# Second norm under the out projection, splits under the merge, solved rows copied by VectorE, inverses in runs of four, HGRN keys a step ahead

## The chip, the cores and the metric

The kernel runs on one core of a Trainium2 chip. The metric is the device time of one execution in microseconds (us): the median of three runs. One execution was also taken with the hardware profiler; the rows further down come from it. Engines: PE (TensorE, matrix products), DVE (VectorE), ACT (ScalarE), POOL (GpSimd), and SP, which here only issues DMAs from its queue.

## The reference, cut to what matters

One layer of a hybrid decoder for 1024 prompt tokens and 8 sample sequences of one token, model width 1024:

```python
h = _rms_norm(x, norm_mix_g)
p_rwkv, p_hgrn, p_gate = split(h @ w_in)          # 1792 | 2048 | 2048 columns
o_a = rwkv7_mixer(p_rwkv)       # 8 heads of 64, delta-rule matrix state, token by token
o_b = hgrn2_mixer(p_hgrn)       # 4 heads of 128, gated linear recurrence, chunks of 64
gate_a, gate_b = split(sigmoid(p_gate))
x = x + (gate_a * (o_a @ w_up_a) + gate_b * (o_b @ w_up_b)) @ w_out
h = _rms_norm(x, norm_ffn_g)
x = x + (silu(h @ w_ffn_gate) * (h @ w_ffn_up)) @ w_ffn_down
y = _rms_norm(x, norm_final_g)
```

The outputs are y for prompt and samples and the new states of both mixers.

## The kernel before, in words

**Data.** Activations stand transposed: 128 channels in the partitions, tokens along the free dimension. The tokens go through in two halves, half 0 with 512 tokens and half 1 with 512 and the 8 samples (520, in two pieces of 260). A tile of 128 channels by one half is the unit; eight of them are the model width (`KD` is 8).

**A dense product.** Precision comes from a split: a tile or a weight is written as high part plus low part (`split`: a copy by ACT rounds the high part, DVE or POOL subtracts for the low one), and `mm3` makes three products of each pair, high by high, low by high and high by low. A weight tile is loaded by `wload`: a DMA that SP issues, ACT's copy `wh`, POOL's subtraction `wl` in four pieces of 256 columns. A 128 x 260 product over eight tiles of the model width is thus 24 matmuls.

**Order of the work.** The program is written as generators. `push` puts a weight's products at the end of a stream of dense work; `start` adds a generator of other work (a chain of a mixer, a norm). `drive` takes the other work's step that is due first, and wherever that step is still waiting it runs one `dense_step` of the stream in the gap. `finish_stream` runs the rest of the stream without other work. Each `yield` is thus a place into which dense work may come. The framework's scheduler then sets each engine's instructions in one fixed order; an engine waits at the first instruction that is not ready.

**Mixers.** Each half has eight RWKV heads in pairs and four HGRN heads. For RWKV the token-by-token recurrence is solved in chunks: `rwkv_prep` inverts the small triangular matrices of all chunks (14 steps of substitution, two DVE operations each, on tiles with one matrix per partition; the data comes to that form and back by DMAs over DRAM, tiles `x`, `t`, `ubd`, `ebd`, `tbd`), and `rwkv_chain` goes through the chunks one after the other: products, the solved rows `z` of two heads copied from PSUM into one operand (`sz`, the trace's `vsz`), and from this operand the new state. `hgrn_chain` does the same over windows: `token_major` transposes a window's keys and values with two PE transposes and an ACT copy (`kv`), two products give the new state and the outputs.

**Tail of a half.** When the last chains are through, the merge of the half follows: `push_merge` pushes per output tile m the products with both `w_up` weights (four PSUM tiles per m in half 1), which DVE multiplies with the sigmoid gates (loaded by DMA) and adds into `merged[m]`. In half 1 the eight merged tiles are then split in `push_out`, which also pushes the out projection: eight weights `w_out`, per tile two PSUM tiles (`pd`) that DVE adds to x1. ACT squares that sum, and DVE adds the squares up for the norm. `second_norm` turns a half's x1 into the operands of the next stage, a Strassen-like form with sums and differences of quadrants: for each of four pairs of tiles four scalings (with PSUM operand), four sums or differences, and five splits of which POOL subtracts two. `second_norm(0)` runs as other work beside the merge of half 1. Then come the FFN (gate, up, by Strassen-like groups) and the down projection, whose operands and weights use slots of named pools (`gslots`).

## Time and profile before

| | us |
|---|---|
| median of three runs | 1928.99 |
| fastest of them | 1925.67 |
| profiled execution, its own time | 1921.57 |
| its span, first to last instruction | 1919.8 |

| engine | busy us | share |
|---|---|---|
| PE | 1772.6 | 92% |
| DVE | 1078.6 | 56% |
| POOL | 969.0 | 50% |
| ACT | 808.7 | 42% |

PE is the engine with the most work. Its idle time is read by stage: the mixers of half 0 and half 1 fill the first 1094 us of the span, the merge of half 1 runs from there to 1134 us, its out projection to 1198 us, and FFN and down projection to the end. In the rows further down, an entry such as `[13.03 <-ACT w__12090 L160]` says that the engine was idle for 13.03 us before this instruction and that ACT's write of `w__12090` ended that wait. Nearly all operations of DVE, ACT and POOL carry line 160, that of the wrapper that issues them, so they are told apart by the tiles' names. The granted clock is a share of TensorE's 2.4 GHz: 1.00 is that, 0.50 is 1.2 GHz.

### The profile page before, as it was taken

The numbers are of one execution on the slowest core, as the hardware profiler recorded it, in microseconds if no ns is written. First come the engines' busy times: TensorE is split into PE (matmuls) and PEld (weight loads), VectorE is DVE, ScalarE is ACT, GpSimd is POOL, SyncE is SP. The second block draws the span as 40 slices with busy tenths as digits, with TensorE's granted clock in tenths as the row PEclk, the third lists the DMA queues.
The fourth block names the chain that finished last, engine by engine and source line by source line (L and its number), as shares of the span: only waits on it lengthen the run. The fifth ranks groups of instructions, "written<-read, shape, count | busy, mean of one in ns | idle before, by whom it ended". The sixth has DMA issues, their size and how long they took to land. (4 is left out here: it accounts for less than half of the span.)

```text
span 1919.8 us, 32939 instructions
## 1 busy us (share of the span) xinstructions
PE 1772.6 (92%) x12376; PEld 1628.9 (85%) x12376; DVE 1078.6 (56%) x2315; ACT 808.7 (42%) x1601; POOL 969.0 (50%) x1131
## 2 busy tenths in 40 slices
PE   6998999988799799899889869999999999999997
PEld 5776778778678789788889769999999999889987
DVE  4476577657465366567554593856656665531214
ACT  4446556656342456354344453433333333421111
POOL 6545555645365456556364364654434343542342
PEclk9998999999899899889989889999999999999998
DMA  4233233343444225323434543123221322732212
GB/s 133 87 72 98 84 81 84 113 131 112 150 161 126 76 66 88 103 70 95 124 114 129 175 156 130 67 89 105 72 84 67 103 75 95 253 109 56 72 52 89
DMA packets 172304, 199.05 MB, mean 104 GB/s; under 512 B 99632, under 2 KB 108080, under 8 KB 172144
## 3 DMA queue, kind: packets, MB, share of 16 engines
q1 hardware_dynamic: 172144, 196.94, 34.3%
q8 instruction: 97, 1.59, 0.4%
q14 instruction: 63, 0.52, 0.1%
HBM read 156.30 MB, written 40.07 MB: 102 GB/s over the span
## 5 line engine op out<-in xcount | busy, mean ns | idle before, releaser
L160 ACT ACT_TABLE_LOAD x66 | 84.7, 1283 | 1.8 <-PEq L1825 0.7
L160 POOL TENSOR_TENSOR d__20102<-d__20102,d__20103 128x512 f32<-128x512 f32 (+1 forms) x14 | 14.2, 1016 | 21.3 <-ACT d__20103 L160 21.3
L160 DVE SCALAR_TENSOR_TENSOR w__6304<-p__6021,vec,pm__6305 128x512 f32<-128x512 f32 x1 | 0.7, 747 | 21.2 <-PE pm__6305 L238 21.2
L238 PE MATMUL pd__12144<-w__12090,wh__12128 128*128 128x260 f32 x1 | 0.6, 584 | 13.0 <-ACT w__12090 L160 13.0
L160 POOL TENSOR_TENSOR wl__1389<-w__1386,wh__1388 128x256 fp32r<-128x256 f32 x4 | 3.2, 841 | 17.0 <-ACT wh__1388 L160 17.0
L160 POOL COPY own<-wkv_st 64x64 f32<-64x64 f32 x16 | 6.2, 386 | 10.7 <-PE pm__4635 L238 3.3
L238 PEld LDWEIGHTS pd__12144<-w__12090,wh__12128 128*128 128x128 f32 x1 | 0.3, 288 | 13.2 <-ACT w__12090 L160 13.2
L160 POOL TENSOR_TENSOR wl__11476<-w__11473,wh__11475 128x256 fp32r<-128x256 f32 x4 | 3.7, 940 | 14.3 <-ACT wh__11475 L160 14.3
L238 PE MATMUL pm__219<-ones,t__196 128*128 128x1 f32 x4 | 1.0, 357 | 9.5 <-DVE t__196 L160 9.5
L160 POOL TENSOR_TENSOR wl__5125<-w__5122,wh__5124 128x256 fp32r<-128x256 f32 x4 | 3.6, 936 | 11.3 <-ACT wh__5124 L160 11.3
L160 POOL TENSOR_TENSOR wl__10054<-w__10051,wh__10053 128x256 fp32r<-128x256 f32 x4 | 2.8, 736 | 12.7 <-ACT wh__10053 L160 12.7
L160 POOL TENSOR_TENSOR wl__3944<-w__3941,wh__3943 128x256 fp32r<-128x256 f32 x4 | 3.3, 855 | 11.8 <-ACT wh__3943 L160 11.8
L238 PEld LDWEIGHTS pm__219<-ones,t__196 128*128 128x128 f32 x4 | 0.9, 322 | 9.5 <-DVE t__196 L160 9.5
L160 POOL TENSOR_TENSOR wl__12202<-w__12199,wh__12201 128x256 fp32r<-128x256 f32 x4 | 2.8, 734 | 11.2 <-ACT wh__12201 L160 11.2
L238 PE MATMUL pm__6333<-t__6313,ebd 128*128 128x128 f32 x8 | 2.1, 441 | 6.6 <-ACT t__6313 L160 6.6
L238 PEld LDWEIGHTS pm__6333<-t__6313,ebd 128*128 128x128 f32 x8 | 1.8, 328 | 6.8 <-ACT t__6313 L160 6.8
L238 PE MATMUL pm__5093<-w__4985,wh__5071 128*128 128x512 f32 x1 | 0.8, 792 | 7.3 <-ACT w__4985 L160 7.3
L160 POOL TENSOR_TENSOR wl__10209<-w__10206,wh__10208 128x256 fp32r<-128x256 f32 x4 | 2.8, 733 | 8.7 <-ACT wh__10208 L160 8.7
L160 POOL TENSOR_TENSOR wl__6274<-w__6271,wh__6273 128x256 fp32r<-128x256 f32 x4 | 2.8, 719 | 8.7 <-ACT wh__6273 L160 8.7
L160 POOL TENSOR_TENSOR wl__1106<-w__1103,wh__1105 128x256 fp32r<-128x256 f32 x4 | 5.1, 1291 | 4.0 <-ACT wh__1105 L160 4.0
L160 POOL TENSOR_TENSOR wl__11397<-w__11394,wh__11396 128x256 fp32r<-128x256 f32 x4 | 2.8, 732 | 7.9 <-ACT wh__11396 L160 7.9
L238 PE MATMUL pc__7693<-vsz__7629,kbt__7700 128*128 128x128 f32 x2 | 0.8, 500 | 6.4 <-ACT vsz__7629 L160 6.4
(23703 smaller groups left out, 8520.1 us busy)
## 6 DMA issues: line engine op xcount, KB each, us to landing
tbd<-t SPq DMA_DIRECT2D x32, 32.0 KB
w__166<-in_w_in SPq DMA_DIRECT2D x1, 512.0 KB
w__184<-in_w_in SPq DMA_DIRECT2D x1, 512.0 KB
w__452<-in_w_in SPq DMA_DIRECT2D x1, 512.0 KB
w__461<-in_w_in SPq DMA_DIRECT2D x1, 512.0 KB
w__501<-in_w_in SPq DMA_DIRECT2D x1, 512.0 KB
w__541<-in_w_in SPq DMA_DIRECT2D x1, 512.0 KB
w__581<-in_w_in SPq DMA_DIRECT2D x1, 512.0 KB
```

The costliest lines, as they stand in the source:

```text
L160: return f(*args, **kw)
L238: PE.matmul(out, lhsT, rhs, start=start, stop=stop)
```

## The change

Five things are moved; the counts of instructions stay, except that 64 copies 64 x 64 pass from ACT to DVE, and that ACT loads its function table 69 times where it was 66.

1. `rwkv_prep` yields after every second step of an inverse's substitution (runs of four DVE operations) in place of every fifth.
2. `rwkv_chain` has both copies of `z` done by DVE; one was ACT's.
3. `hgrn_chain` issues the transposes and the copy of the next window's keys and values right behind this window's products, without a step of its own.
4. In half 1 each merged tile is split as soon as its merge ends, into slots of pool `h` that are free by then, and the out projection follows at once. The sums of squares of half 0 stay beside the merge, while `second_norm(0)` runs beside the out projection of half 1.
5. The operands of the second norm and the down projection's tiles use other slots for that.

```diff
@@ -776,7 +776,7 @@
                 ALU.mult,
             )
             V.tensor_tensor(n3[:, 0:q, q + 1 : 16], n3[:, 0:q, q + 1 : 16], tv, ALU.add)
-            if q % 5 == 0:
+            if q % 2 == 0:
                 yield
         V.memset(nb[:, 0:256:17], 1.0)
         d2 = dp.tile([4 * nblk, 256], F32, tag="d2", name=nm("d2"))
@@ -924,8 +924,8 @@
                 kbt1 = token_major(c + 1)
             yield
             mm(z, tbd[:, c], d_)
-            V.tensor_copy(sz[HEADS[0], 1, 0], z[HEADS[0], 0])
-            A.activation(sz[HEADS[1], 1, 1], z[HEADS[1], 1], AF.Copy)
+            for h in range(2):
+                V.tensor_copy(sz[HEADS[h], 1, h], z[HEADS[h], h])
             yield
             mm(ds, kbt, sz[:, 1])
             for h in range(2):
@@ -1183,6 +1183,8 @@
             if s0 is not None:
                 mm(py, qe[:, wc], s0, True, False)
             mm(py, at[:, w], kv[:, 1], s0 is None, True)
+            if w + 1 < NWIN:
+                kv = token_major(w + 1)
             if s0 is None:
                 V.tensor_copy(sn, po[:, :P])
             else:
@@ -1192,9 +1194,6 @@
             V.scalar_tensor_tensor(at[:, w], yr[:, wc], 1.0, yr[:, wc], ALU.mult, ALU.mult, accum_out=ss[:, w : w + 1])
             s0 = sn
             yield
-            if w + 1 < NWIN:
-                kv = token_major(w + 1)
-                yield
         if half == 1:
             SP.dma_start(out=o["hgrn_p"][hd], in_=s0)
         u["y"] = yr, ss
@@ -1268,7 +1267,7 @@
             for b in range(2):
                 item(m, b)
 
-    def push_merge(m, half, src, gates, merged):
+    def push_merge(m, half, src, gates, merged, done=None):
         def body(w):
             y = merged[m]
             gs = [slot(HLEN[half], tag="t") for _ in range(2)]
@@ -1283,7 +1282,7 @@
                     V.tensor_tensor(g[:, sl], g[:, sl], ps, ALU.mult)
                 V.tensor_tensor(y[:, sl], gs[0][:, sl], gs[1][:, sl], ALU.add)
 
-        push(i["w_up"][m], body)
+        push(i["w_up"][m], body, done)
 
     def add_to(y):
         return lambda sl, ps: V.tensor_tensor(y[:, sl], y[:, sl], ps, ALU.add)
@@ -1361,7 +1360,9 @@
         mh, ml, rest = many(half, F32R)
         for m in range(KD):
             split(merged[m], mh[m], ml[m])
-
+        push_out_of(half, mh, ml, x1, done)
+
+    def push_out_of(half, mh, ml, x1, done=None):
         def item(m):
             push(
                 i["w_out"][m],
@@ -1371,7 +1372,6 @@
 
         for m in range(KD):
             item(m)
-        return mh + ml + rest
 
 
     xs = [slot(HP) for _ in range(KD)]
@@ -1444,8 +1444,9 @@
         pools[tag], bufs[tag], widths[tag] = fp, FSLOTS[tag], HP + NS
 
     merged = [slot(HLEN[1], tag="p") for _ in range(KD)]
+    mh, ml = h_slots(1)
     for m in range(KD):
-        push_merge(m, 1, src, s["gates"], merged)
+        push_merge(m, 1, src, s["gates"], merged, lambda m=m: split(merged[m], mh[m], ml[m]))
 
     x1 = [slot(HP, tag="p") for _ in range(3)]
     for _ in range(2):
@@ -1453,8 +1454,6 @@
     x1.append(slot(HP, tag="n"))
     for m in range(KD):
         SP.dma_start(out=x1[m], in_=x1d[m])
-    h2t = [[slot(HP, F32R, "h") for _ in range(16)] + [slot(HP, F32R, tag=y) for y in "w" * 11 + "n"], None]
-
     def operands(tiles, half):
 
         n = HLEN[half] // 2
@@ -1465,7 +1464,7 @@
         ops["B11"] = [[t[:, part * n : part * n + n] for t in tiles[6::7]] for part in range(2)]
         return ops
 
-    def second_norm(half, x1, acc, tiles):
+    def second_norm(half, x1, acc, tiles, b12=None):
         n = HLEN[half] // 2
         rs = rstd(acc, half)
         yield
@@ -1492,20 +1491,28 @@
             split(b1, h2, l2, G)
             yield
 
+    acc0 = slot(HP, tag="t")
+
+    def sums():
+        add = square_sum(acc0)
+        for k in range(KD):
+            add(x1[k])
+            yield
+
+    start("norm", sums())
+    drive()
+    finish_stream()
+
+    h2t = [[slot(HP, F32R) for _ in range(SLOTS["w"])], None]
+    for _ in range(2):
+        h2t[0] += parts_of(double(F32R), HP + NS)
+    for _ in range(2):
+        h2t[0] += parts_of(triple(F32R), HP + NS)
+    rest = h2t[0][7 * KD // 2 :]
+    h2t[0] = [y[:, :HP] for y in h2t[0][: 7 * KD // 2]]
     h2s = [operands(h2t[0], 0), None]
     b12 = [slot(HP, F32R, "s") for _ in range(KD // 2)]
-
-    def first_second_norm():
-        acc = slot(HP, tag="t")
-        add = square_sum(acc)
-        for k in range(KD):
-            add(x1[k])
-            yield
-        yield from second_norm(0, x1, acc, h2t[0])
-
-    start("norm", first_second_norm())
-    drive()
-    finish_stream()
+    x1_first = x1
     x1 = load_x(1, "pppppppp")
     x1e = dp.tile([KD, P, HLEN[1]], F32, tag="x1e", name="x1e", bufs=1)
     acc1 = slot(tag="n")
@@ -1516,10 +1523,13 @@
         for f, (a, b) in zip(add, CHUNKS[1]):
             f(x1[m][:, a:b])
 
-    h2t[1] = push_out(1, merged, x1, residual)
+    push_out_of(1, mh, ml, x1, residual)
+    start("norm", second_norm(0, x1_first, acc0, h2t[0], b12))
+    drive()
+    h2t[1] = mh + ml + rest
     for _ in range(2):
         h2t[1] += parts_of(double(F32R), HLEN[1])
-    h2t[1] += [slot(HLEN[1], F32R, "n") for _ in range(6)]
+    h2t[1] += [slot(HLEN[1], F32R, "n") for _ in range(7)]
 
 
 
@@ -1669,10 +1679,10 @@
                 yield from ts
 
     gslots = (
+        (("w", 16),),
+        (("h", 16), ("d", 8), ("n", 4)),
+        (("w", 19), ("a", 6), ("n", 3)),
         (("h", 16),),
-        (("n", 7), ("w", 13), ("d", 8)),
-        (("h", 16), ("w", 6), ("a", 6)),
-        (("w", 13), ("n", 3)),
     )
     x1s = [[slot(HP, tag="p") for _ in range(KD)], [slot(tag=y) for y in "pppttttt"]]
     f0s = [sum(FGROUPS[:g]) for g in range(len(FGROUPS))]
```

The order of the instructions on each engine shows what becomes of that at three places.

The first is the seam between the merge and the out projection of half 1. On PE before, `pd__12023` is the merge's last product, `pd__12144`, `pd__12170` and `pd__12208` are tiles of the out projection, and `w__12090` is the first merged tile's high part:

```order
L238 MATMUL pd__12023<-a__11298,wh__11886 128x260 x2
L238 MATMUL pd__12023<-a__11298,wl__11887 128x260
L238 MATMUL pd__12144<-w__12090,wh__12128 128x260
L238 MATMUL pd__12170<-w__12090,wh__12128 128x260
L238 MATMUL pd__12208<-w__12090,wh__12137 128x260
L238 MATMUL pd__12144<-w__12091,wh__12128 128x260
L238 MATMUL pd__12144<-w__12090,wl__12129 128x260
```

PE now; `pd__11973` is the merge's last product, `pm__12035` the sum of squares of half 0 and `pd__12062` the first out tile:

```order
L238 MATMUL pd__11973<-a__11298,wh__11851 128x260 x2
L238 MATMUL pd__11973<-a__11298,wl__11852 128x260
L238 MATMUL pm__12035<-ones,t__11367 128x1 x4
L238 MATMUL pd__12062<-h__11337,wh__12046 128x260
L238 MATMUL pd__12062<-h__11345,wh__12046 128x260
L238 MATMUL pd__12062<-h__11337,wl__12047 128x260
L238 MATMUL pd__12062<-h__11338,wh__12046 128x260
L238 MATMUL pd__12062<-h__11346,wh__12046 128x260
L238 MATMUL pd__12062<-h__11338,wl__12047 128x260
L238 MATMUL pd__12062<-h__11339,wh__12046 128x260
```

The sum over half 0 has come from the middle of the merge to its end, and the out tiles take eight `h` tiles. DVE before at this seam (`d__12098` to `w__12093` are merged tiles' low parts, 128x256 and 128x512 the second norm):

```order
L160 TENSOR_TENSOR d__11340<-n__11342,d__11340 128x256
L160 TENSOR_TENSOR d__11340<-t__12055,n__11342 128x256
L160 TENSOR_TENSOR d__12098<-p__11333,d__12098 128x520
L160 TENSOR_TENSOR w__11373<-t__12055,w__11372 128x512
L160 TENSOR_TENSOR d__12099<-p__11334,d__12099 128x520
L160 TENSOR_TENSOR a__12100<-p__11335,a__12100 128x520
L160 TENSOR_TENSOR w__12091<-p__11329,w__12090 128x520
L160 TENSOR_TENSOR a__12101<-p__11336,a__12101 128x520
L160 TENSOR_TENSOR w__12093<-p__11330,w__12092 128x520
```

DVE now (`h__11351` is the seventh merged tile's low part):

```order
L160 TENSOR_TENSOR h__11351<-p__11335,h__11343 128x520
L160 TENSOR_TENSOR t__11925<-t__11925,pd__11944 128x260
L160 TENSOR_TENSOR p__11336<-t__11924,t__11925 128x260
L160 TENSOR_TENSOR t__11924<-t__11924,pm__11959 128x260
L160 TENSOR_TENSOR t__11925<-t__11925,pd__11973 128x260
L160 TENSOR_SCALAR ms__12040<-pm__12035 128x4
L160 TENSOR_TENSOR p__11336<-t__11924,t__11925 128x260
L160 TENSOR_TENSOR h__11352<-p__11336,h__11344 128x520
L160 SCALAR_TENSOR_TENSOR p__11353<-p__11353,vec,pm__12071 128x512
```

The low parts stand between the merge's own operations, where of the second norm only the scaling of its sums (`ms__12040`) is left. The eighth tile's low part (`h__11352`) is followed by the norm's scalings.

The second place is SP's queue at the first inverse of the second half, before (`w1202__6271` is a weight of the input projection, `t320`, `ubd`, `t1197` and `tbd0` are the inverse's way over DRAM):

```order
L160 DMA vs1248__6495<-smp1247__6489 128x8x1
L160 DMA t320_105<-x_1172__6041 16x4x16 x8
L160 DMA ubd_100<-t320_105 32x4x32 x4
L160 DMA t1197__6202<-t320_105 128x4x32
L160 DMA tbd0_97<-t320_105 32x8x32 x4
L160 DMA w1202__6271<-in_w_in 128x1024
L160 DMA w1225__6379<-in_w_in 128x1024
```

SP's queue now:

```order
L160 DMA vs1235__6453<-smp1234__6447 128x8x1
L160 DMA w1201__6257<-in_w_in 128x1024
L160 DMA t320_105<-x_1180__6144 16x4x16 x8
L160 DMA ubd_100<-t320_105 32x4x32 x4
L160 DMA tbd0_97<-t320_105 32x8x32
L160 DMA t1213__6312<-t320_105 128x4x32
L160 DMA tbd0_97<-t320_105 32x8x32 x3
L160 DMA w1214__6343<-in_w_in 128x1024
```

The weight that follows `w1185` (now `w1201__6257`) stands ahead of the inverse's sixteen DMAs, no longer behind them.

The third is PE at the first half's tail, before; `pd__5009` is the last tile of the input projection, `pm__5093` the merge:

```order
L238 MATMUL pd__5009<-h__4427,wl__4875 128x260
L238 MATMUL pd__5009<-h__4428,wh__4874 128x260
L238 MATMUL pd__5009<-h__4436,wh__4874 128x260
L238 MATMUL pd__5009<-h__4428,wl__4875 128x260
L238 MATMUL pm__5093<-w__4985,wh__5071 128x512
L238 MATMUL pm__5093<-w__4986,wh__5071 128x512
L238 MATMUL pm__5093<-w__4985,wl__5072 128x512
L238 MATMUL pm__5137<-w__4985,wh__5080 128x512
```

PE now; `kv__4974` and `kv__4991` are keys and values of the last HGRN chain's last two windows, `pm__5016` the tail's transposes:

```order
L238 MATMUL pm__4985<-hs__4967,w__4311 128x128
L238 MATMUL pm__4985<-kv__4974,w__4310 128x128
L242 MATMUL pm__4988<-cst,w__4312 128x128
L242 MATMUL pm__4988<-cst,p__3464 128x128
L242 MATMUL pm__4996<-cst,w__4024 128x128 x4
L238 MATMUL pm__5004<-kv__4991 128x128
L238 MATMUL pm__5006<-hs__4984,w__4311 128x128
L238 MATMUL pm__5006<-kv__4991,w__4310 128x128
L242 MATMUL pm__5016<-cst,w__4945 128x128 x4
L238 MATMUL pm__5093<-w__5024,wh__5071 128x512
```

Where 48 matmuls of the input projection stood between the last HGRN chain and the merge, the chain's last four windows and the transposes now stand with no dense tile between them.

## Rows read from the trace of the kernel before

**Rows 1.** The page, part 1: busy us (share of the span) x instructions.

```profile
PE 1772.6 (92%) x12376; PEld 1628.9 (85%) x12376; DVE 1078.6 (56%) x2315; ACT 808.7 (42%) x1601; POOL 969.0 (50%) x1131
```

**Rows 2.** Busy time by windows: width, engines' busy us, granted clock, DMA share, GB/s.

```profile
1094.00:1133.70 39.70, 38.83 (x316) 38.04 (x316) 34.26 (x65) 21.61 (x35) 29.78 (x32) 1.00 0.47 154
1137.00:1154.10 17.10, 5.47 (x23) 5.17 (x24) 15.64 (x23) 8.04 (x15) 8.88 (x8) 0.50 0.55 182
1160.20:1197.60 37.40, 37.40 (x316) 37.40 (x314) 15.08 (x26) 11.17 (x19) 19.71 (x27) 1.00 0.38 131
1232.00:1908.00 676.00, 671.68 (x5130) 647.07 (x5128) 335.84 (x570) 206.08 (x357) 295.62 (x263) 1.00 0.29 94
```

**Rows 3.** Timeline, PE at the seam: start, us, engine, line, operation [idle <-releaser].

```profile
1146.71 0.58 PE L238 MATMUL pd__12144<-w__12090,wh__12128 128*128 128x260 f32 x1 [13.03 <-ACT w__12090 L160]
...
1149.65 0.58 PE L238 MATMUL pd__12144<-w__12091,wh__12128 128*128 128x260 f32 x1 [1.92 <-DVE w__12091 L160]
```

**Rows 4.** Timeline, DVE, 1131 to 1153 us.

```profile
1131.08 1.52 DVE L160 TENSOR_TENSOR t__12038<-p__11339 128x256 f32<-128x256 f32 x1
1132.52 0.41 DVE L160 TENSOR_TENSOR t__11894<-t__11894,pd__11953 128x260 f32<-128x260 f32 x1
...
1136.00 0.68 DVE L160 TENSOR_TENSOR h__11366<-t__12038,h__11365 128x512 fp32r<-128x512 f32 x1
1136.61 0.73 DVE L160 SCALAR_TENSOR_TENSOR d__11340<-d__11340,vec,pm__11740 128x512 f32<-128x512 f32 x1
...
1145.39 0.69 DVE L160 TENSOR_TENSOR d__12098<-p__11333,d__12098 128x520 fp32r<-128x520 f32 x1
...
1151.95 0.69 DVE L160 TENSOR_TENSOR w__12097<-p__11332,w__12096 128x520 fp32r<-128x520 f32 x1
```

**Rows 5.** Timeline, POOL and ACT, 1130 to 1147 us.

```profile
1130.88 1.44 POOL L160 TENSOR_TENSOR w__11370<-d__11341,w__11369 128x512 fp32r<-128x512 f32 x1 [1.01 <-ACT w__11369 L160]
...
1146.04 0.62 ACT L160 ACTIVATE w__12090<-p__11329 128x520 fp32r<-128x520 f32 x1
```

**Rows 6.** Timeline, DVE and POOL in the steady out projection.

```profile
1165.96 0.43 DVE L160 TENSOR_TENSOR p__12076<-p__12076,pd__12276 128x260 f32<-128x260 f32 x1 [0.70 <-PE pd__12276 L238]
...
1166.87 0.67 DVE L160 TENSOR_TENSOR n__12089<-n__12089,t__12329 128x260 f32<-128x260 f32 x1 [0.49 <-ACT t__12329 L160]
...
1170.00 3.01 POOL L160 TENSOR_TENSOR wl__12338<-w__12335,wh__12337 128x256 fp32r<-128x256 f32 x4 [2.74 <-ACT wh__12337 L160]
```

**Rows 7.** Timeline, DVE and ACT, one step's two copies of solved rows.

```profile
737.03 0.21 DVE L160 COPY vsz__7153<-pc__7471 64x64 f32<-64x64 f32 x1
...
740.85 0.22 ACT L160 ACTIVATE vsz__7153<-pc__7471 64x64 f32<-64x64 f32 x1
```

**Rows 8.** Timeline, SP's queue, ACT and PE, the second half's first inverse.

```profile
616.90 11.90 SPq L160 DMA_DIRECT2D t<-x__6041  x8
...
634.13 0.38 SPq L160 DMA_DIRECT2D w__6271<-in_w_in  x1
...
637.97 1.06 ACT L160 ACTIVATE wh__6273<-w__6271 128x1024 fp32r<-128x1024 f32 x1 [10.50 <-DMA w__6271<-in_w_in]
...
642.18 2.08 PE L238 MATMUL pm__6333<-t__6313,ebd 128*128 128x128 f32 x8 [6.61 <-ACT t__6313 L160]
```

**Rows 9.** Timeline, ACT and PE, the first half's tail.

```profile
494.75 0.63 ACT L160 ACTIVATE t__5175<-t__5175 128x512 f32<-128x512 f32 x1 [5.37 <-DMA t__5175<-gate__2188]
...
496.12 0.79 PE L238 MATMUL pm__5093<-w__4985,wh__5071 128*128 128x512 f32 x1 [7.33 <-ACT w__4985 L160]
```

**Rows 10.** Timeline, PE, two windows of the second half's last HGRN chain.

```profile
1069.90 0.49 PE L238 MATMUL pm__11226<-kv__11224 128*128 128x128 f32 x2
...
1071.58 0.49 PE L238 MATMUL pm__11240<-kv__11238 128*128 128x128 f32 x2
```

**Rows 11.** Busy time by windows, as Rows 2, around the two tails.

```profile
480.00:520.00 40.00, 30.10 (x149) 23.69 (x148) 16.62 (x28) 13.21 (x22) 15.16 (x19) 0.87 0.42 132
1060.00:1094.00 34.00, 25.57 (x153) 22.83 (x151) 14.12 (x37) 12.17 (x24) 7.85 (x8) 0.75 0.60 196
```

More of the change, by code (lines that the diff above doesn't have):

```diff
@@ L1493, in second_norm @@
             yield
-    h2s = [operands(h2t[0], 0), None]
-    b12 = [slot(HP, F32R, "s") for _ in range(KD // 2)]
-    def first_second_norm():
-        acc = slot(HP, tag="t")
-        add = square_sum(acc)
+    acc0 = slot(HP, tag="t")
+    def sums():
+        add = square_sum(acc0)
         for k in range(KD):
@@ L1503, in first_second_norm @@
             yield
-        yield from second_norm(0, x1, acc, h2t[0])
-    start("norm", first_second_norm())
+    start("norm", sums())
     drive()
     finish_stream()
+    h2t = [[slot(HP, F32R) for _ in range(SLOTS["w"])], None]
[5 more added lines that the diff above has]
+    h2t[0] = [y[:, :HP] for y in h2t[0][: 7 * KD // 2]]
+    h2s = [operands(h2t[0], 0), None]
+    b12 = [slot(HP, F32R, "s") for _ in range(KD // 2)]
+    x1_first = x1
     x1 = load_x(1, "pppppppp")
```

## The prediction

> **What bounds the kernel now.** I read the page's shares first. PE is busy for 1772.6 of 1919.8 us [rows 1], so only some 147 us can be won by better order; the rest is matrix work, and the change leaves that as it is. Next come the windows. From 1232 to 1908 us PE is busy for 671.68 of 676 us at clock 1.00 [rows 2], so FFN and down projection can hardly gain. The loss lies ahead of that: in the mixers, at the two tails, and at the seam between the merge and the out projection of half 1. The merge has PE busy for 38.83 of 39.70 us, the steady out projection for all of its 37.40 us; between them PE waits 13.03 us for the first split tile and 1.92 us for its low part [rows 2, 3]. After that wait it also runs slowly: from 1137.0 to 1154.1 us the granted clock is 0.50 [rows 2]. A PE that has stood idle is thus paid for twice, by the wait and by slower matmuls behind it. What is late there is DVE: busy for 15.64 of these 17.10 us [rows 2], with the second norm and then with eight low parts, the first at 1145.39, the last at 1151.95 us [rows 4]. ACT's first high part comes only at 1146.04 us [rows 5].
>
> **The seam, part 4.** *What it costs now.* The steady out projection does 13 PSUM tiles in 37.40 us, 2.88 us each [rows 2]. The three tiles ahead of 1160.2 us should take 8.6 us, but from the merge's end at 1133.7 they take 26.5. The seam costs 17.9 us.
>
> *What remains.* The low parts move into the merge: 8 x 0.69 = 5.5 us of DVE and 8 x 0.62 = 5.0 us of ACT [rows 4, 5]. The second norm leaves the merge, so there is room. The last merged tile is ready an addition, a high part and a low part after the last matmul, some 2 us; meanwhile PE has the products of seven tiles, 21 matmuls or 2.5 us. The spread of the norm's factor waits for POOL and is short. I take 1 us for all of this.
>
> *What the second norm costs in its new place.* PE needs 16 x 2.88 = 46 us for the stage. DVE needs 16 evacuations of 0.43 = 6.9 and 15 additions of 0.67 = 10.1 us [rows 6], eight scalings of 0.73 and, four times, six operations of 0.41 and one of 0.68 [rows 4], 18.4 us. The sum is 35.4 us, under 46. POOL needs eight weights at 3.01 [rows 6] and nine subtractions at 1.44 [rows 5], 37 us, also under 46. But the norm's work is ready at the start and bunches there, in front of evacuations for which PE waits, so PE may stall 0 to 5 us; I take 2. The seam's 17.9 less 3 is a gain of **15 us**. Lower bound of the gain 5, upper 18.
>
> *A rule that speaks against it.* DVE slows beside POOL: a 128 x 256 operation with both inputs in SBUF that starts at 1131.08, while POOL runs from 1130.88 for 1.44 us, takes 1.52 us and ends after POOL does, but one with a PSUM input takes 0.41 us at 1132.52 [rows 4, 5]. The Trainium skill, "SBUF — State Buffer", section "Who interferes with whom", says that a DVE instruction with two SBUF inputs and a GpSimd instruction that reads SBUF exclude each other, and that the second to issue blocks fully; the trace agrees in this pair of rows. If that holds for the whole stage, POOL's 37 us and DVE's two-SBUF operations (15 x 0.41 + 4 x (5 x 0.41 + 0.68) = 17 us) may not overlap: 54 us against 46, some 8 to 10 us longer. That is rival A. I don't forecast it because the merge holds 34.26 us of DVE and 29.78 of POOL in 39.70 us while PE hardly stalls [rows 2].
>
> **The inverse, part 1.** An inverse gets seven yields in place of two, so more dense work is laid between. At the second half's first inverse, SP's queue takes 11.90 us to issue the inverse's stores and issues the next weight at 634.13; ACT stands 10.50 us for this weight, and PE then 6.61 us for what is queued behind it on ACT [rows 8]. In the new order that weight is issued ahead of the stores. ACT's wait should go, and with it PE's 6.61 and some slow matmuls: **-7 us**, bounds 0 (the next weight is late instead) and -11. The other inverses show no PE wait of that size.
>
> **The solved rows, part 2.** DVE's copy takes 0.21 us and ACT's 0.22 [rows 7], but they don't start together: in the row's step ACT's comes 3.82 us later, because ACT has large operations ahead of it. Over the sixteen places where PE waits for ACT's copy, of which this is the widest, ACT is later by 5.4 us together. DVE does two in 0.42 us, so some 0.2 is given back per step where PE waits. **-3 us**, bounds 0 and -6. DVE gets 64 x 0.21 = 13 us more, beside 1078.6 of 1919.8 [rows 1]; where DVE itself is late a copy can wait longer than on ACT, hence the zero.
>
> **HGRN keys, part 3.** A window without stall takes 1.68 us on PE (1069.90 to 1071.58) [rows 10], of which its two groups of products are under 0.9; bare, it leaves PE idle for 0.8 us. In the new order most windows follow each other with less dense work between. Transposes and ACT's copy are off the chain, so most still find cover: **+3 us**, bounds 0 and, with half of the 32 windows bare, +12.
>
> **The two tails.** They move because dense work is consumed elsewhere: more in the inverses, so that the chains come later in it. In half 0 the 48 matmuls (5.8 us at 2.88 per 24) that stood between the last HGRN chain and the merge are gone, and the chain's last four windows lie bare: 4 x 0.8 = 3.3 us. The wait before the first merge product was 7.33 us [rows 9], set by ACT, which stood 5.37 us for a gate's DMA; it loses its cover and I take 10 to 11. Together **+7 us**, bounds +3 and +12. In half 1 there is the reverse: 48 gate matmuls now stand between the last windows and the tail's transposes. Before, PE was busy for 25.57 of the 34 us from 1060, at clock 0.75 [rows 11]. 5.8 us of cover for these 8.4 idle us: **-5 us**, bounds 0 and -9.
>
> **Costed at nothing.** Three more table loads on ACT (42% busy [rows 1]); the slots of the down projection, under a PE that is full [rows 2], +-2 us if a slot comes free late.
>
> **Sum.** -15 - 7 - 3 + 3 + 7 - 5 = -20 us against the profiled execution's own 1921.57: 1901.6. That execution is 4.1 us below the fastest timed one and 7.4 below the median, so in the terms of the timed runs I forecast **1906 us**. Of the six terms' bounds not all fall to one side; half of each combined as independent gives about +-12: 1894 to 1918.
>
> **Rivals.**
> *A, DVE and POOL block each other in the out projection* (above): the seam gives 5, not 15. For it speaks the 1.52 us; against it the merge stage, which bears both. Time 1916.
> *B, slower: the first half's dense work runs out.* The dense stream that covers chains is one stock: seven yields per inverse eat it early, and the late chains lie bare. Half 0's tail then costs the 5.8 us of lost cover, 6.7 for four bare windows and some 3 for slow matmuls behind them (5.47 busy us at half clock lose 2.7 at the seam [rows 2]), 15.5; the other windows their +12; and the first inverse's -7 is lost to later inverses. Against these 27.5 stand -15, -5 and -3: 5 us slower, 1931, and more where chains wait for each other. It decides from 23 us of new stalls in the mixers on. For it speaks the new order, in which no dense tile is left at that place, and PE's 30.10 of 40 us there already [rows 11]; against it that the same dense work still covers something earlier.
> *C, everything comes off at its upper bound*, with mixers that stall less because inverses are spread out: -18 - 11 - 6 - 9 + 4 = -40, 1887.
> *D, it doesn't do what it says:* the norm's bunch delays PE as long as the splits did, 13 to 15 us, and the other terms cancel: 1925.
>
> **Chances.** Forecast 0.46, A 0.18, B 0.15, C 0.13, D 0.08. The range that leaves out half of C and the upper half of B, and little else, is **1886 to 1932**. 2%, about what a measurement of this kernel can tell from no change, is 38.6 us of 1928.99: 1890.4 and 1967.6. Faster by more: about two thirds of C and the forecast's low end, 0.14. Slower by more: a far end of B, 0.03. Within: 0.83.
>
> **What would show it.** The seam: PE's longest wait at the start of the out projection under 2 us, clock 1.00 through it, and the stage at 46 to 51 us; with A, evacuations late and PE waits of about a microsecond at several out tiles, the stage at 54 us or over. The inverse: no wait of ACT over 3 us for a weight there. The copies: PE's waits for `vsz` ended by DVE, shorter in sum. The tails: a wait before the first merge product of half 0 of 10 us, and in half 1 less than 4 us idle. The prediction is wrong if the mixers' idle time moves by more than 15 us either way, or if the seam's stall only changes its place.

## The result

The changed kernel takes 1936.59 us (median of 19 runs), the kernel before 1924.66 beside it. The ratio is 1.0058, 95% interval 1.0044 to 1.0072: slower by 11 us, where I forecast 1% faster and a range up to 1932. That is less than the 2% that I had called the least a measurement can tell, but with 19 executions of each kernel the interval leaves no doubt of the sign. Executions that took far longer than the others of their kernel (2442.92 us once here; 2470 and 4770 us, two of the six of e5) are not in the ratios.

The profiled execution of the changed kernel has a span of 1931.9 us. Its page, part 1, answers to [rows 1]:

```profile
PE 1789.8 (93%) x12376; PEld 1640.9 (85%) x12376; DVE 1105.4 (57%) x2379; ACT 795.5 (41%) x1540; POOL 968.9 (50%) x1131
```

PE has the same 12376 matmuls and is busy for 17 us more: part of its work ran at the lower clock. To see where, both kernels are cut at the same events: the first merge product of half 0; the first merge product of half 1 that reads RWKV heads (called its first merge product below; products of its HGRN heads come from 1063.4 us on before, from 1096.3 now); the last merge product; the end of the out projection. The second stretch, called half 1's mixers, also holds half 0's merge and out projection. Columns as in [rows 2]. Before:

```profile
0.00:496.10 496.10, 443.86 (x2508) 370.68 (x2508) 304.46 (x752) 269.93 (x558) 272.65 (x386) 0.98 0.35 100
496.10:1079.30 583.20, 524.34 (x3728) 481.74 (x3728) 332.34 (x808) 270.81 (x585) 312.55 (x390) 0.94 0.40 111
1079.30:1133.70 54.40, 49.96 (x373) 47.93 (x373) 39.95 (x77) 24.43 (x39) 31.06 (x33) 0.91 0.49 161
1133.70:1197.60 63.90, 48.97 (x388) 48.67 (x388) 34.86 (x56) 22.32 (x39) 32.08 (x39) 0.87 0.39 131
```

After:

```profile
0.00:525.40 525.40, 462.08 (x2509) 385.28 (x2509) 313.64 (x785) 262.10 (x528) 275.24 (x392) 0.94 0.34 96
525.40:1101.40 576.00, 524.59 (x3728) 483.41 (x3728) 347.23 (x840) 263.25 (x550) 309.40 (x384) 0.93 0.40 110
1101.40:1154.10 52.70, 47.35 (x360) 45.10 (x360) 33.00 (x63) 24.17 (x36) 25.03 (x28) 0.94 0.53 177
1154.10:1207.10 53.00, 48.85 (x406) 48.05 (x404) 43.76 (x70) 24.72 (x46) 39.78 (x42) 1.00 0.47 158
```

The out projection with its seam gained 10.9 us (63.9 to 53.0) and runs at clock 1.00. Half 1's mixers gained 7.2, the merge 1.7. Half 0's mixers lost 29.3 us with the same number of matmuls, 11 of them as more idle time and 18 as slower matmuls (443.86 to 462.08 us busy). The stages behind, to the end, took 722.2 and now 724.8 us.

These are single executions, and their noise can be read: up to this merge the changed kernel and e2 below have the same order of instructions on PE, DVE, ACT and POOL, and so have the kernel before, e1 and e17, and e8 and e18. Executions of one order differ by up to 5.4 us in half 0 and by 2.2, 5.9 and 12.3 us in half 1's mixers. The 29.3 us stand clear of that, the 7.2 don't.

**The seam.** PE now starts the first out tile 0.65 us after the merge, where [rows 3] had 13.03 us. Later its two longest waits are for a PSUM tile that DVE evacuates late. Timeline of the changed kernel, PE, DVE and POOL:

```profile
1154.75 0.37 PE L238 MATMUL pd__12062<-h__11337,wh__12046 128*128 128x260 f32 x1
...
1177.67 0.39 PE L238 MATMUL pd__12327<-h__11337,wh__12209 128*128 128x260 f32 x1 [1.03 <-DVE p__12021 L160]
...
1182.71 0.36 PE L238 MATMUL pd__12380<-h__11337,wh__12294 128*128 128x260 f32 x1 [1.89 <-DVE p__12021 L160]
...
1173.67 0.41 DVE L160 TENSOR_TENSOR a__12012<-d__11356,a__12012 128x256 fp32r<-128x256 f32 x1
1174.00 1.51 DVE L160 TENSOR_TENSOR t__12225<-d__11357,t__12225 128x256 f32<-128x256 f32 x1
1175.44 1.51 DVE L160 TENSOR_TENSOR p__11354<-d__11357,p__11354 128x256 f32<-128x256 f32 x1
...
1177.20 0.41 DVE L160 TENSOR_TENSOR p__12021<-p__12021,pd__12216 128x260 f32<-128x260 f32 x1
...
1173.78 1.45 POOL L160 TENSOR_TENSOR a__12012<-n__11358,a__12011 128x512 fp32r<-128x512 f32 x1 [0.66 <-ACT a__12011 L160]
1175.19 1.47 POOL L160 TENSOR_TENSOR s__13014<-r__13008,s__13013 128x512 fp32r<-128x512 f32 x1
```

The evacuation of `p__12021` stands behind DVE operations that take 1.51 us each and end 0.28 us after the POOL operation beside them; one of the same shape that starts before POOL's takes 0.41 us. This is rival A's picture [rows 4, 5].

**Half 0.** From 300 to 490 us fewer matmuls fit into the same time, at a lower clock. Windows of before, then of after:

```profile
300.00:490.00 190.00, 175.55 (x1116) 153.13 (x1114) 122.12 (x308) 114.74 (x251) 105.32 (x131) 0.99 0.39 113
```

```profile
300.00:490.00 190.00, 171.77 (x995) 148.30 (x994) 127.67 (x304) 108.00 (x225) 99.64 (x121) 0.92 0.33 99
```

121 matmuls (11%) are missing there. Dense products were used earlier: of half 0's 1392, 625 have started by 200 us, before 575; by 350 us the changed kernel is behind (947 and 958), and the last one comes at 501.0 us for 488.8. The tail follows, bare of dense products (timeline of after, ACT and PE):

```profile
505.73 0.63 ACT L160 ACTIVATE t__5175<-t__5175 128x512 f32<-128x512 f32 x1 [9.06 <-DMA t__5175<-gate__1974]
...
508.29 0.38 ACT L160 ACTIVATE kv__4950<-pm__4947 128x256 f32<-128x256 f32 x1
...
501.82 0.27 PE L242 MATMUL pm__4947<-cst,p__3464 128*128 128x128 f32 x1
508.72 0.80 PE L238 MATMUL pm__4952<-kv__4950 128*128 128x128 f32 x2 [6.62 <-ACT kv__4950 L160]
...
511.49 0.79 PE L238 MATMUL pm__4965<-kv__4960 128*128 128x128 f32 x2 [0.47 <-ACT kv__4960 L160]
...
516.75 0.63 PE L238 MATMUL pm__4982<-kv__4974 128*128 128x128 f32 x2
...
519.52 0.48 PE L238 MATMUL pm__5004<-kv__4991 128*128 128x128 f32 x2
...
524.00 1.12 PE L242 MATMUL pm__5016<-cst,w__4945 128*128 128x128 f32 x4 [2.72 <-DVE w__4945 L160]
525.38 0.79 PE L238 MATMUL pm__5093<-w__5024,wh__5071 128*128 128x512 f32 x1 [0.26 <-ACT w__5024 L160]
```

In [rows 9] ACT's wait for a gate held only the merge's start; here ACT stands 9.06 us for a gate with the last chain's key copy queued behind it. Then the last four windows (`pm__4952` to `pm__5004`) start 2.8, 5.3 and 2.8 us apart. From the last dense product (501.0) to the merge it is 24.4 us, before 7.3.

**First inverse of half 1.** The 6.61 us of [rows 8] are gone, but now ACT waits for the next weight and PE, a little later, for what stands behind it on ACT:

```profile
667.75 1.06 ACT L160 ACTIVATE wh__6345<-w__6343 128x1024 fp32r<-128x1024 f32 x1 [6.15 <-DMA w__6343<-in_w_in]
...
669.34 0.49 PE L238 MATMUL pm__6291<-cst,rx__6366 128*128 128x128 f32 x2 [4.45 <-ACT rx__6366 L160]
```

### The profile page after: what moved, and what is told of

Read it like the earlier page. It is cut to its first block, busy times and chain, and to the rows that moved or that the text cites. A ratio compares the mean times of both kernels' runs of the same rounds, so it can differ in the third digit from the quotient of the medians.

```text
span 1931.9 us, 33037 instructions
## 1 busy us (share of the span) xinstructions
PE 1789.8 (93%) x12376; PEld 1640.9 (85%) x12376; DVE 1105.4 (57%) x2379; ACT 795.5 (41%) x1540; POOL 968.9 (50%) x1131
## 5 line engine op out<-in xcount | busy, mean ns | idle before, releaser
L160 POOL TENSOR_TENSOR wl__5125<-w__5122,wh__5124 128x256 fp32r<-128x256 f32 x4 | 3.6, 929 | 18.2 <-ACT wh__5124 L160 18.2
L160 POOL TENSOR_TENSOR wl__11462<-w__11459,wh__11461 128x256 fp32r<-128x256 f32 x4 | 3.7, 954 | 16.4 <-ACT wh__11461 L160 16.4
L160 POOL TENSOR_TENSOR wl__3049<-w__3046,wh__3048 128x256 fp32r<-128x256 f32 x4 | 4.8, 1224 | 5.7 <-ACT wh__3048 L160 5.7
L160 POOL TENSOR_TENSOR wl__9750<-w__9747,wh__9749 128x256 fp32r<-128x256 f32 x4 | 3.7, 948 | 7.7 <-ACT wh__9749 L160 7.7
L160 POOL TENSOR_TENSOR wl__7157<-w__7154,wh__7156 128x256 fp32r<-128x256 f32 x4 | 3.8, 980 | 6.8 <-ACT wh__7156 L160 6.8
L160 POOL TENSOR_TENSOR wl__3709<-w__3706,wh__3708 128x256 fp32r<-128x256 f32 x4 | 4.7, 1191 | 4.9 <-ACT wh__3708 L160 4.9
L160 POOL TENSOR_TENSOR wl__3880<-w__3877,wh__3879 128x256 fp32r<-128x256 f32 x4 | 3.3, 850 | 7.5 <-PE pd__3887 L238 7.5
L160 POOL TENSOR_TENSOR wl__5081<-w__5078,wh__5080 128x256 fp32r<-128x256 f32 x4 | 3.0, 774 | 7.8 <-ACT wh__5080 L160 7.8
L160 POOL TENSOR_TENSOR wl__11702<-w__11699,wh__11701 128x256 fp32r<-128x256 f32 x4 | 3.5, 898 | 6.8 <-ACT wh__11701 L160 6.8
L160 POOL TENSOR_TENSOR wl__9321<-w__9318,wh__9320 128x256 fp32r<-128x256 f32 x4 | 2.8, 725 | 8.0 <-ACT wh__9320 L160 8.0
L160 POOL TENSOR_TENSOR wl__1893<-w__1890,wh__1892 128x256 fp32r<-128x256 f32 x4 | 2.8, 737 | 7.2 <-ACT wh__1892 L160 7.2
```

The lines of the kernel that those rows point to most:

```text
L160: return f(*args, **kw)
```

## The experiments

Ratios are to the kernel before on the same chip. **Theory S**: the dense products are one stock; inverses with seven yields use it up early in half 0, and late chains and tail lie bare. **Rival Z**: the second copy on DVE makes the chains wait.

**e1: parts 4 and 5 alone** (the change's hunks from `push_merge` on):

```diff
+        push_merge(m, 1, src, s["gates"], merged, lambda m=m: split(merged[m], mh[m], ml[m]))
...
+    push_out_of(1, mh, ml, x1, residual)
+    start("norm", second_norm(0, x1_first, acc0, h2t[0], b12))
```

> Parts 4 and 5 alone on the kernel before: splits under the merge, second norm under the out projection, new slots. From the changed kernel's trace (last merge product to the end of the out projection 55.8 us, before 63.9) every theory expects about 8 us less than before, ratio 0.995 to 0.997; the mixers keep their order and their times (first merge product of half 0 at 496 us). If the norm's new place cost something later, the ratio would be 1.000 or over.

Ratio 0.9947 (0.9927 to 0.9968), 10 us faster, just beyond the expected 0.995; first merge product at 498.3 us. From the last merge product to the end of the out projection it is 53.4 us, 10.5 less than before: the seam is worth what its stage shows. The profiled execution, the slowest of the six, is no shorter as a whole: its mixers took 8 us more, in the old order.

**e2: parts 1 to 3 alone**, the complement:

```diff
+            if q % 2 == 0:
...
+            for h in range(2):
+                V.tensor_copy(sz[HEADS[h], 1, h], z[HEADS[h], h])
...
+            if w + 1 < NWIN:
+                kv = token_major(w + 1)
```

> Parts 1 to 3 alone (inverses in runs of four, both copies by VectorE, HGRN keys ahead), the complement of the run before. If the parts add up, it must be slower than before by what the changed kernel lost plus the seam's gain: about 11 + 8 = 19 to 22 us, ratio 1.010 to 1.012, with the first merge product of half 0 near 525 us in place of 496. If the loss comes from the late stages, the ratio is 1.000.

Ratio 1.0116 (1.0093 to 1.0140), first merge product at 529.3 us. The whole loss lies in the three mixer parts; e1 and e2 add up to the change (-10 and +22).

**e3: part 1 alone.**

```diff
-            if q % 5 == 0:
+            if q % 2 == 0:
```

> Part 1 alone: yields after every second step of an inverse. Theory S (the stock of dense work runs out): the inverses use up the dense products early, none stands under the last HGRN chain of half 0, the tail lies bare; first merge product at 515 to 530 us, ratio 1.006 to 1.012. Rival Z (the second copy on VectorE makes the chains wait): this run has no such copy, the ratio is 0.997 to 1.000 and the first merge product comes by 500 us.

Ratio 1.0058 (1.0039 to 1.0077), a hair under the expected 1.006; first merge product at 515.5 us. Half 0 takes 19.4 us more, half 1's mixers 5.9 less, which is no more than executions of one order differ by. The window from 300 to 490 us, as above:

```profile
300.00:490.00 190.00, 170.75 (x996) 147.63 (x996) 124.30 (x293) 112.77 (x244) 96.22 (x123) 0.91 0.34 101
```

It is the changed kernel's window without DVE's copies: theory S holds for part 1.

**e4: the change without part 1.**

```diff
-            if q % 2 == 0:
+            if q % 5 == 0:
```

> The changed kernel with part 1 undone (yields after every fifth step again); parts 2 to 5 stay. Theory S: 230 dense matmuls stand from the last HGRN chain of half 0 on, the tail is covered, the first merge product comes at 490 to 500 us, and the whole takes 12 to 20 us less than before, ratio 0.990 to 0.994. Rival Z: the copies and the HGRN steps still make the chains wait, first merge product after 510 us, ratio 1.003 to 1.008.

Ratio 0.9946 (0.9927 to 0.9965). The bare tail is gone, yet the merge starts at 512.1 us, a miss: parts 2 and 3 lengthen half 0 too. Half 1's mixers take 576.6 us. So S is not all, and the two parts had to be run apart.

**e5: part 2 alone. e6: part 3 alone.**

```diff
-            V.tensor_copy(sz[HEADS[0], 1, 0], z[HEADS[0], 0])
-            A.activation(sz[HEADS[1], 1, 1], z[HEADS[1], 1], AF.Copy)
+            for h in range(2):
+                V.tensor_copy(sz[HEADS[h], 1, h], z[HEADS[h], h])
```

> Part 2 alone on the kernel before: both copies of the solved rows by VectorE. Theory S (dense stock; the copies matter little): ratio 0.998 to 1.001. Rival Z (VectorE, loaded further, makes the chains wait): ratio 1.004 to 1.008, with PE's waits that DVE ends in half 0 up from 19 us to over 35 us, as in the changed kernel without part 1 (42 us).

```diff
             mm(py, at[:, w], kv[:, 1], s0 is None, True)
+            if w + 1 < NWIN:
+                kv = token_major(w + 1)
...
-            if w + 1 < NWIN:
-                kv = token_major(w + 1)
-                yield
```

> Part 3 alone on the kernel before: keys of the next HGRN window made a step ahead, one yield less per window. If parts 2 and 3 lose half 0's 14 us (which the run without part 1 lost against parts 4 and 5 alone) through this part, ratio 1.003 to 1.007 and first merge product of half 0 after 505 us; if through the copies, 0.996 to 1.000 and before 500 us.

e5: 1.0189 (1.0169 to 1.0210). e6: 1.0218 (1.0198 to 1.0237). Both are far outside every expectation: 36 and 42 us alone, and with e3's 11 they make 90 where the three together (e2) lose 22. Costs that belong to the parts don't behave so. What such a stall looks like in e6 (timeline, PE, DVE, POOL):

```profile
926.10 0.79 PE L238 MATMUL pm__9209<-hs__9156,w__7908 128*128 128x128 f32 x2 [11.20 <-DVE hgrn_st L160]
...
925.09 0.69 DVE L160 TENSOR_TENSOR w__9182<-w__9182,w__9183 128x512 f32<-128x512 f32 x1 [10.62 <-POOL w__9183 L160]
925.70 0.34 DVE L160 SCALAR_TENSOR_TENSOR hgrn_st<-hs__9156,ebc__8837,pm__9207 128x128 f32<-128x128 f32 x1
...
917.59 2.35 POOL L160 TENSOR_SCALAR w__9191<-cst,dst__9136 128x128 f32<-128x128 f32 x4 [3.84 <-DMA out__445<-w__9051]
...
924.02 1.04 POOL L160 TENSOR_TENSOR w__9183<-w__9183,w__7030 128x512 f32<-128x512 f32 x1
```

The chain's state update of 0.34 us stands on DVE behind an operation of the samples, which waits 10.62 us for POOL; POOL has stood 3.84 us for a DMA and has other operations ahead. PE's wait ends with this update, not with the keys (another product had read `kv__9163` at 913.56 us): the order put it behind that operation. Why this product needs the update is not shown.

**e7 and e8: parts 4 and 5 with part 1, and with parts 1 to 3, in half 1 alone.**

```diff
+            if q % (2 if half else 5) == 0:
...
+            if half:
+                V.tensor_copy(sz[HEADS[1], 1, 1], z[HEADS[1], 1])
+            else:
+                A.activation(sz[HEADS[1], 1, 1], z[HEADS[1], 1], AF.Copy)
```

> Parts 4 and 5, and part 1 in half 1 alone (half 0's instructions on PE in the order of the kernel before). Theory S: in half 0 the inverses eat the stock, in half 1 the gate products of the dense stream last; so half 0 stays at 496 to 500 us and half 1's mixers fall from 589 to about 578 us: ratio 0.988 to 0.991, 10 us under parts 4 and 5 alone. If runs of four cost by themselves (more switching of DVE between chains), half 1 is 589 us or longer and the ratio 0.995 or more.

> Parts 4 and 5, and parts 1 to 3 in half 1 alone. The changed kernel's half 1 took 576.0 us and its stages behind that 823.3 us; with half 0 as before (496 to 500 us) the theory expects the sum of these, about 1897 us from the first to the last instruction, ratio 0.986 to 0.990, the fastest so far. If half 1 gained only because half 0 left it other work, the ratio is 0.994 or more.

e7: 0.9898 (0.9872 to 0.9924); half 0 at 501.3 us, half 1's mixers 579.8. e8: 0.9897 (0.9874 to 0.9920); 499.6 and 576.8. Both came out as theory S said: without the runs of four half 0 keeps its time. That they gain in half 1 rests on 0.5% between e1 and e7, one order each, which is no more than e11 and e12 below bring. The 823.3 us in e8's expectation run to the last matmul only; to the last instruction they are 830.5, the sum is 1904, and e8's span was 1906.0.

**e9 to e12: the engine against the order.** **Theory P**: a part acts through the order that the program's planner lays (it adds up its own costs per operation and puts dense work where a step still waits), not through its own operations. For e9 DVE copies while the planner counts ACT's cost and queue; for e10 the reverse:

```diff
+    class ByVector:
+        def activation(self, out, x, func):
+            return nc.vector.tensor_copy(out, x)
+
+    AV = Clocked(ByVector(), "A")
...
-            A.activation(sz[HEADS[1], 1, 1], z[HEADS[1], 1], AF.Copy)
+            AV.activation(sz[HEADS[1], 1, 1], z[HEADS[1], 1], AF.Copy)
```

> Both copies by VectorE as in part 2, but the program's planner is told ACT's cost and queue for the second one, so the order of the work is almost that of the kernel before (101 lines of PE's order differ, with part 2 alone 1116). Theory P (part 2 costs through the order that the planner lays, not through VectorE): ratio 0.996 to 1.002. Rival Z (the copy waits on VectorE): ratio 1.010 to 1.019 as with part 2 alone.

> The reverse: the second copy stays on ACT, but the planner is told VectorE's cost and queue, so the order is nearly that of part 2 alone (78 lines of PE's order differ from it). Theory P: ratio 1.014 to 1.022, as slow as part 2 alone. Rival Z: 0.998 to 1.003.

e9: 0.9967 (0.9953 to 0.9982). e10: 1.0140 (1.0118 to 1.0163). Mixers of half 0 and half 1 in e9, then e10:

```profile
0.00:498.00 498.00, 444.20 (x2509) 372.49 (x2509) 317.11 (x784) 263.06 (x526) 273.61 (x386) 0.97 0.34 100
498.00:1074.20 576.20, 518.58 (x3728) 476.56 (x3728) 345.07 (x840) 262.38 (x553) 310.41 (x390) 0.95 0.39 112
```

```profile
0.00:515.40 515.40, 453.63 (x2508) 379.09 (x2508) 308.82 (x751) 270.22 (x559) 267.38 (x386) 0.96 0.32 96
515.40:1109.40 594.00, 531.29 (x3728) 489.65 (x3728) 324.76 (x807) 276.36 (x589) 314.07 (x389) 0.93 0.40 109
```

DVE's copies (x784 operations against x752 in half 0) gain 6 us under nearly the old order; the new order loses 27 us with DVE's load as before (x751). Rival Z's sign of long waits for DVE did come in e5: in half 0 PE waits 41.0 us for it. But e10, with 27.4 us of such waits, idles as long there (61.8 us, e5 62.2, before 52.2). So Z falls as the cause of part 2's loss. The two shares don't add up, though: -6 and +27 make 21, and e5 lost 36. Whether the copies or the 78 lines of PE's order that differ make e5 0.5% slower than e10 the runs don't tell.

```diff
-DMA_US, DMA_ELEMENT_US, ISSUE_US, HOP_US = 2.2, 0.00002, 0.45, 0.25
+DMA_US, DMA_ELEMENT_US, ISSUE_US, HOP_US = 2.2, 0.00002, 0.45, 0.26
```

> The kernel before with one constant of its planner changed: what it adds to each operation for the hop to the next engine is 0.26 us for 0.25. No instruction is added, removed or given to another engine; 465 lines of PE's order differ. Theory P: a difference this small re-lays the mixers, and the time moves clearly, by 0.3 to 2% to either side. If the order is robust and parts 2 and 3 really cost what they took, the ratio is 0.998 to 1.002.

> As the run before with 0.24 us for the hop; 491 lines of PE's order differ. Theory P: the time moves by 0.3 to 2% to either side, and the two runs needn't lie on opposite sides of the kernel before. Otherwise 0.998 to 1.002.

e11: 1.0037 (1.0021 to 1.0053). e12: 1.0050 (1.0030 to 1.0070). A change of 0.01 us in a constant that no instruction contains costs 7 to 10 us, by the order alone.

**e13: part 3 with its yields kept** (beside the two lines that e6 adds):

```diff
             s0 = sn
             yield
             if w + 1 < NWIN:
-                kv = token_major(w + 1)
                 yield
```

> Part 3 alone, but with a yield kept behind each window, so that the planner can lay dense work at as many places as before; the keys of the next window are still issued ahead. Theory Y (part 3 alone loses 2.2% through the missing yields, which let the windows follow each other too closely): ratio 0.995 to 1.004. Rival K (the keys' copy ahead of the window's own copy on ACT, or any other order that the planner draws): ratio 1.010 or more.

1.0078 (1.0060 to 1.0095), between the two. With the yields kept, 1.4 of the 2.2% are gone. That the yields themselves cost this is not shown: the arbitrary change of e16 below also brings 1.4%, those of e11 and e12 about half of the remaining 0.8%.

**e14: e7 with e9's copies.**

> Parts 4 and 5, part 1 in half 1 alone, and both copies by VectorE under the old plan. If the two that were measured alone add up (0.9898, and 0.9967 for the copies): ratio 0.984 to 0.988, the fastest of all. If VectorE is full where half 1's inverses run: 0.990 or more.

0.9969 (0.9953 to 0.9986): they do not add up. VectorE being full is not shown either: the mixers took 501.0 and 579.1 us in the profiled execution, level with e7. Even that says little, since this execution was the fastest of its twelve and e7's the slowest of its six. Open.

**e15 and e16: the changed kernel with the hop at 0.26 and 0.24 us** (edit as in e11).

> The changed kernel with the planner's hop at 0.26 us for 0.25, nothing else. Theory P (the changed kernel's time against before is one draw of an order out of many): its ratio to before leaves 1.0058 by more than 0.003, to 0.995 to 1.020, with the seam's part unchanged (the stages behind the first merge product of half 1 stay at 822 to 826 us). If the parts cost what they took, the ratio stays at 1.004 to 1.008.

> The same with 0.24 us. Theory P: a ratio that leaves 1.0058 by more than 0.003, and not the same as with 0.26; the stages behind the first merge product of half 1 stay at 822 to 826 us. Otherwise 1.004 to 1.008.

e15: 1.0076 (1.0059 to 1.0092), inside the 1.004 to 1.008 of the other side, so a miss for theory P. e16: 1.0202 (1.0182 to 1.0221), 28 us over the changed kernel. From the first merge product of half 1 to the last matmul they take 824.9 and 829.0 us (the latter 3 more than expected), against 823.3: the difference lies in the mixers, and there in half 1, whose mixers take 586.5 and 606.3 us against 576.0. Half 0's merge starts at 521.0 and 519.0 us against 525.4, in e16 without a bare tail (8.5 us from the last dense product), so the tail alone doesn't make half 0's loss.

**e17 and e18: POOL's part of the norm under the out projection given to DVE**, in e1 and in e8:

```diff
-            split(b2, h3, l3, G)
+            split(b2, h3, l3, G if half else V)
...
-            split(b1, h2, l2, G)
+            split(b1, h2, l2, G if half else V)
```

> Parts 4 and 5 alone, with the eight subtractions of half 0's second norm that POOL does under the out projection given to VectorE (PE's order is the same, line by line). Theory L (VectorE's operations of 1.5 us there wait for POOL's, and that makes the evacuations late, 1.9 + 1.1 us of PE waits): VectorE's 256-column operations fall from 1.5 to 0.4 us, it has eight more of 0.7 = 5.6 us but gives back about eight times 1.1, the two PE waits go, and the out projection is 2 to 4 us shorter than in the run of parts 4 and 5 alone (ratio 0.993 to 0.995 against 0.9947, at the edge of what can be told; the profile decides). Rival: VectorE is simply too full there; then its waits grow and the stage is longer.

> Parts 4 and 5, parts 1 to 3 in half 1 alone (0.9897), and the norm's eight subtractions by VectorE as in the run beside it. Theory L: 0.987 to 0.990, the fastest version or level with it; the rival: 0.991 or more.

e17: 0.9942 (0.9925 to 0.9959), which alone can't be told from e1. The stage can: the out projection's window of e1, then of e17, with PE's order the same:

```profile
1141.30:1194.00 52.70, 49.37 (x397) 48.77 (x397) 42.74 (x68) 24.08 (x45) 39.75 (x42) 0.97 0.47 158
```

```profile
1137.50:1186.90 49.40, 48.27 (x397) 47.36 (x397) 43.09 (x76) 23.80 (x45) 29.90 (x34) 1.00 0.47 166
```

DVE does eight operations more (x68 to x76) and is busy for only 0.35 us more, since its own are shorter: of the 24 with 256 columns and no PSUM input, five took 1.5 us in e1 and one does in e17. PE's two waits for DVE, 1.9 and 1.1 us in e1, are gone (the longest is now 0.6), and for a weight's low part from POOL, which is freed too, PE had not waited in e1. The stage is 3.3 us shorter. Of all runs with parts 4 and 5, the eight with POOL's share in place take 52.9 to 53.4 us from the last merge product to the end of the out projection, e17 and e18 both 50.1. e18: 0.9865 (0.9841 to 0.9888), 1891.07 us, the fastest: 1.35% under the kernel before and 1.9% under the change. Part of its lead over e8 is one execution's mixers (494.2 and 564.6 us), which a new order of half 0's norm can't explain; the intervals of e8 and e18 overlap.

**Half 0 in all runs.** The start of half 0's merge sorts the twenty profiled executions. It lies at 494.2 to 501.3 us in the ten that have none of parts 1 to 3 in half 0 or, as e9, nearly the old order, and at 511.3 to 529.3 us in the ten that have one of them there or, as e10, its order. The planner's constant moved it by 4 to 6 us (e11 and e12 from before, e15 and e16 from the change). So each part brings a loss there, alone or with others, though the losses don't add up. Whether any other re-laying as large (1116 lines of PE's order for part 2, against 465 and 491 in e11 and e12) would lose as much is not shown. Half 1's mixers, 564.6 to 611.4 us, fall into no such groups.

## Why the prediction was wrong

**The step that failed** is the pricing of parts 1 to 3. I took each as a local edit in an order that stays: a copy that moves, keys off the chain, one inverse, two tails, -5 us together. They lose 22 us together (e2), and the place is half 0's mixers, 29.3 us in the change. e10 shows why the price of a copy said nothing: its engine is worth -6 us (e9), at the bound I gave for part 2; the order that comes with it is worth +27. Part 3, priced at +3 with a bound of +12, takes 42 us alone. That the plan as a whole would be re-laid I had not priced at all; in half 0 all ten runs with such an order lost. My sign for it was blind as well: I watched the mixers' idle time, and it moved by +11.1 us in half 0 and -7.5 in half 1, under the 15 that I had set, while 18 us came as matmuls at a lower clock (0.94 for 0.98).

**Rival B had the mechanism for part 1.** The stock runs out in half 0: e3 puts the merge 19.4 us later, and e7 saves this by leaving half 0 alone. B's 1931 was near, with 27.5 us of new stalls for half 0's 29.3; I gave it 0.15. The tail was mis-sized: I took its wait from 7.33 to 10 or 11 us with a bound of +12 for the whole. It is 24.4 us from the last dense product to the merge: ACT's wait for a gate came to hold the chain's key copy and not only the merge's start, for which PE stood 6.62 us, and the bare windows follow each other at 2.8 to 5.3 us where I had 1.68 and 0.8 of it idle. And I looked at the tail alone, where the last dense product already came 12.2 us later.

**The seam** was right in kind. I forecast 15 us less, with bounds 5 and 18; the stage gained 10.9 and the runs 10.2 (e1). The mis-sized term is DVE in the norm's new place: I took 2 us and a stage of 46 to 51, it is 52.4 from the first out matmul. Rival A gave 54 for this. The Trainium skill, "SBUF — State Buffer", section "Who interferes with whom", has DVE's operations with two SBUF inputs and GpSimd's that read SBUF shut each other out; e17 agrees, where 9.9 us less of POOL's work lets DVE do eight operations more in nearly the same busy time. My argument against it, that the merge bore both loads, weighed too much. The merge of [rows 2] has 35 DVE operations without a PSUM input beside POOL's 32, and two of them took 1.5 us as well, and PE's longest wait there is 0.7 us; the changed out projection has 44 beside 42, five of them at 1.5 us, and there evacuations stand behind them.

**The smaller terms.** The copies: PE's waits for `vsz` in the mixers are now ended by DVE, as forecast, but not shorter in sum (28.6 us before, 29.7 in the change; 23.3 in e9). The first inverse: right that PE's 6.61 us go, with 4.45 us of a new wait behind the next weight, the bound I had named. Half 1's mixers gained 7.2 us in the change, 5.9 in e3, which single executions can't tell from nothing. The second tail gained about 2 us of idle time of the 5 forecast: in the 34 us laid around the merge's start as in [rows 11], PE idles 6.3 us for 8.4 (my sign was under 4), at clock 0.90 for 0.75. Down projection and table loads: nothing, as said (722.2 and 724.8 us to the end). The sum's last step has a slip: 1906 is counted from the fastest timed run; from the median, which is the metric, it is 1909.

**Open**: what makes one order better than another. The traces show single cases (e6), no rule that would rank orders beforehand, and for parts 2 and 3 no common reason for half 0's loss: in e4, e6 and e13 dense products last until the merge, and it is late all the same. Open too is why e14 does not add up.

## What to carry to other kernels

Where a planner or scheduler lays the order from estimated costs, an edit's own duration is not its price: change a constant of the planner by a hair first, see how far the time moves (here up to 28 us), and treat any smaller effect of an edit as unproven until engine and order have been separated as in e9 and e10, or until one stage shows it in several executions, as half 0 and the out projection do here. Dense work that covers latencies is a stock; look at where it ends after the edit, over the whole last third and not only at the tail. A seam with an idle matrix engine is the safe gain, if the work moved there does not make two vector engines wait for each other.

## What the runs showed of the hardware

A short wait can cost more behind it than in itself. In the changed kernel PE is busy at clock 1.00, then waits 3.19 us, and the granted clock then stays at half (1.2 GHz) for 17 us, with PE busy nearly throughout:

```profile
320.02 0.39 PE L238 MATMUL pd__3098<-h__144,wh__3048 128*128 128x512 f32 x1
320.25 0.39 PE L238 MATMUL pd__3098<-h__136,wl__3049 128*128 128x512 f32 x1
...
325.46 1.41 PE L238 MATMUL pm__3117<-a__3033,d__3034 64*128 64x128 f32 x5 [3.19 <-DVE a__3033 L160]
...
338.34 0.63 PE L238 MATMUL pd__3189<-h__134,wh__3090 128*128 128x512 f32 x1
338.77 0.63 PE L238 MATMUL pd__3189<-h__142,wh__3090 128*128 128x512 f32 x1
```

```profile
320.00:322.50 2.50, 2.27 (x10) 1.50 (x8) 2.47 (x4) 2.42 (x4) 1.35 (x4) 1.00 0.33 134
325.00:342.50 17.50, 17.04 (x59) 13.79 (x60) 12.04 (x21) 1.54 (x2) 5.87 (x6) 0.51 0.25 58
342.50:345.00 2.50, 2.50 (x17) 2.19 (x16) 0.13 (x1) 0.00 (x0) 0.59 (x1) 1.00 0.37 46
```

Of the 59 matmuls in these 17.5 us, 19 are dense products of 512 columns; they start 0.43 us apart (338.34, 338.77), before the wait 0.23 (320.02, 320.25). The length of the wait doesn't tell what follows: behind the 11.20 us in e6 the clock is back at 1.00 after 3.7 us (926.1 to 929.8). What makes the difference the runs don't show.
